# Twenty load widths instead of eleven in a masked softmax

## The chip, the cores and the metric

The kernel runs on one core of one Trainium2 chip. The metric is the device time of one execution in microseconds (us).

## The reference

```python
batch, heads, seq_q, seq_k = 16, 8, 256, 256
x       = randn(batch, heads, seq_q, seq_k)             # float32
lengths = randint(seq_k // 2, seq_k, size=batch)        # 128 to 255

for b in range(batch):
    masked = x[b, :, :, :lengths[b]]
    masked = masked - max(masked, axis=-1)
    e = exp(masked)
    result[b, :, :, :lengths[b]] = e / sum(e, axis=-1)  # the other columns are 0
```

Each batch has 2048 rows of 256 columns, 2 MB. Only the first `lengths[b]` columns of a row count, so the rest need not be read. The draw is fixed: the lengths of batches 0 to 15 are 188, 233, 229, 243, 195, 252, 165, 210, 222, 180, 209, 157, 159, 199, 214 and 248.

## The kernel before

**Tiling.** A batch is one tile of 128 partitions with 16 rows of 256 columns each. `xt` holds eight such tiles (slots). The work goes through 16 positions; `batch_of` says which batch stands at a position: batches 1, 2, 3 and 15 at positions 0 to 3, batches 4 to 14 at positions 4 to 14, and batch 0 at position 15.

**Loads.** SyncE loads position 0 in two halves. GpSimd loads positions 1 to 3 as whole rows (line 196). Positions 4 to 15 are the narrow loads: a loop of six turns (line 205), each with an even and an odd position (`par`). For each, GpSimd waits until the slot's old contents are stored (`s_st[par]`, line 209), reads the batch's length into a register (line 210), and calls `pick` (line 163). `pick` is a binary tree over the list `widths` with the full 256 columns at its end. Each inner node compares the length with a width (line 173); each leaf waits for the landing of the load before last (`s_sw[par]`, line 167) and then issues a DMA of the first w columns of every row (line 168). So the choice is made ahead of the wait for the landing, and behind the wait for the slot. The tree is written out twice in the loop, once for each parity.

**What is not loaded.** Columns from `low` (160) on are filled with zeros once, in slots 4 to 7 (`fill`, line 190); the others hold older numbers. The mask makes a very negative number of all columns behind the length, so that what stands there doesn't matter.

**Compute.** VectorE masks columns 128 to 255 of a tile (`mask`, `clip`, line 248), ScalarE takes the exponential, in part with row sums (lines 374 and 377), VectorE sums the other rows (`total`, line 269), takes reciprocals (line 279) and multiplies a half tile at a time (line 282). The order on VectorE is written out by hand (lines 289 to 304).

**Stores.** SyncE stores each half tile or quarter when VectorE has multiplied it (lines 146 to 156), always whole rows of 256 columns, so their bytes don't depend on the lengths. The last position's stores count on `s_last`, and SyncE's wait for it (line 407; the profile shows it under line 433) is the last of the program.

**After the loop.** A few small instructions check that all sums were in range (lines 310 to 328); with this draw the second, exact pass behind them is not run.

Of the kernel before, what the change touches and what calls it, by code (L numbers as in the profile page):

```python
# [21 lines left out]
def kernel(  # L22
# [28 lines left out]
        return pos + 1 if pos < ahead - 1 else {ahead - 1: 15, 15: 0}.get(pos, pos)  # L51


    widths = list(range(160, 248, 8))
    low = widths[0]
    mid = seq_k // 2
    big = 1.0e30
# [380 lines left out]
```

## Time and profile before

| | before |
|---|---|
| median of 3 runs | 154.69 us (154.58 to 154.7) |
| profiled execution: span, first to last instruction | 152.8 us |
| the profiled execution's own time beside the span | not on the page |
| VectorE (DVE) busy | 134.6 us, 88% |
| ScalarE (ACT) busy | 95.1 us, 62% |
| GpSimd (POOL) busy | 21.3 us, 14% |
| moved by DMA | 61.57 MB, 403 GB/s over the span |
| read from and written to HBM | 27.98 MB, 33.55 MB |

Engine names in the profile: DVE is VectorE, ACT ScalarE, POOL GpSimd, SPq the queue of SyncE and POOLq that of GpSimd. A row of a group gives line, engine, operation, the tiles, the count and the durations. A row of a wait gives the waiting engine and line, what it waited for, the total in us, the count and the longest. A row of a stage gives the stretch, then the busy time of each engine with the count of instructions, the granted TensorE clock, the busy share of the 16 DMA engines and the GB/s they moved. A row of the timeline gives start and duration in us; in brackets is the idle time ahead of it and what ended it. A row of a DMA queue gives packets, MB and the share of the 16 engines' time. A row of DMA issues gives the count, KB each and the us from issue to landing.

### The profile page before, as it was taken

What the parts mean: (1) busy time and instruction counts of PE and PEld (TensorE: products, weight loads), DVE (VectorE), ACT (ScalarE), POOL (GpSimd) and SP (SyncE); (2) the same over time, 40 slices, a digit from 0 to 9 for tenths busy, and PEclk for the clock granted to TensorE, in tenths of its full rate; (3) what the DMA queues carried; (4) which work ended last, traced back from release to release, by engine and by line L of the source; (5) the groups of instructions that cost most, each with busy time, mean ns of one, the idle gap of its engine ahead of it and who ended that gap; (6) DMA issues with size and microseconds to landing.
All of it is one profiled execution on the core that took longest, in us unless ns stands there. A gap on an engine that the chain in (4) does not pass through costs nothing.

```text
span 152.8 us, 818 instructions
## 1 busy us (share of the span) xinstructions
PE 0.3 (0%) x2; PEld 0.2 (0%) x2; DVE 134.6 (88%) x107; ACT 95.1 (62%) x402; POOL 21.3 (14%) x29
## 2 busy tenths in 40 slices
PE   0000000000000000000000000000000000000000
PEld 0000000000000000000000000000000000000000
DVE  1369999999999999999999999999999999999500
ACT  3096699339394967859393939577593939395000
POOL 4962110030303020030300220302000000000000
DMA  4999999999999999999999999999999999999994
GB/s 107 420 446 433 401 435 347 421 445 420 394 397 422 405 421 411 411 409 405 419 411 418 408 399 419 408 410 423 417 421 419 413 420 422 435 435 442 429 410 187
DMA packets 10646, 61.57 MB, mean 403 GB/s; under 512 B 898, under 2 KB 1010, under 8 KB 7058
## 3 DMA queue, kind: packets, MB, share of 16 engines
q1 hardware_dynamic: 5904, 35.65, 56.7%
q0 software_dynamic: 4736, 25.89, 41.9%
q14 instruction: 4, 0.03, 0.1%
q10 hardware_dynamic: 2, 0.00, 0.0%
HBM read 27.98 MB, written 33.55 MB: 403 GB/s over the span
## 4 chain that ended last, share of the span: by engine, by line
DVE 87%; DMA 5%; issue 1%; SPq 0%; PE 0%
DVE xt L282 48%; DVE xt L248 23%; DVE row_sum L269 12%; DMA xt<-in_x_dram 5%; DVE inv_sum L279 3%; DVE ends L317 0%; SPq L145 0%; DVE bad L320 0%; PE count L218 0%; DVE redo L328 0%; SPq L433 0%; SPq L106 0%
## 5 line engine op out<-in xcount | busy, mean ns | idle before, releaser
L377 ACT ACTIVATE xt<-xt 128x256 f32<-128x256 f32 x192 | 76.6, 400 | 0.2 <-DVE xt L248 0.2
L282 DVE TENSOR_TENSOR xt<-xt,inv_sum 128x2048 f32<-128x2048 f32 x32 | 73.3, 2292 | 1.1
L374 ACT ACTIVATE xt<-xt 128x1024 f32<-128x1024 f32 x16 | 16.9, 1056 | 42.8 <-DVE xt L248 42.8
L248 DVE SCALAR_TENSOR_TENSOR xt<-down,len_s,xt 128x2048 f32<-128x2048 f32 (+1 forms) x17 | 37.7, 2219 | 5.0 <-DMA xt<-in_x_dram 5.0
L377 ACT ACTIVATION_READ_ACCUMULATOR xt<-xt 128x1 f32 x192 | 35.9, 187 | 0.0
L168 POOL DMA_DIRECT2D xt<-in_x_dram x12 | 13.2, 1104 | 84.0 <-DMA xt<-in_x_dram 62.3
L269 DVE TENSOR_REDUCE row_sum<-xt 128x4 f32<-128x1024 f32 x16 | 19.4, 1210 | 0.0
L279 DVE RECIPROCAL inv_sum<-row_sum 128x8 f32<-128x8 f32 x32 | 6.3, 198 | 0.5
L191 POOL MEMSET xt<- 128x1536 f32 x4 | 5.4, 1398 | 1.1 <-DVE len_s L239 1.1
L361 ACT ACT_TABLE_LOAD x1 | 1.3, 1283 | 1.6 <-SPq L106 1.6
L196 POOL DMA_DIRECT2D xt<-in_x_dram x3 | 1.8, 590 | 0.0
L231 DVE TENSOR_SCALAR down<-iota_i 128x256 f32<-128x256 int32 x1 | 0.3, 300 | 1.6 <-POOL iota_i L181 1.6
L317 DVE TENSOR_REDUCE ends<-inv_sum 128x1 f32<-128x256 f32 x2 | 0.7, 408 | 0.0
L236 DVE CAST len_b<-word 1x16 bf16<-1x16 int32 x1 | 0.2, 164 | 0.4 <-DMA word<-in_lengths_dram 0.4
L239 DVE TENSOR_SCALAR len_s<-len_f 128x16 f32<-128x16 f32 x1 | 0.2, 176 | 0.3 <-PE len_f L216 0.3
L218 PE MATMUL count<-bad,ones_c 128*1 128x3 bf16 x1 | 0.2, 165 | 140.8 <-DVE bad L320 140.8
L181 POOL IOTA iota_i<- 128x256 int32 x1 | 0.3, 331 | 0.6 <-SPq L106 0.6
L328 DVE TENSOR_REDUCE redo<-count 1x1 f32<-1x3 f32 x1 | 0.1, 150 | 0.3 <-PE count L218 0.3
L320 DVE TENSOR_SCALAR bad<-ends 128x1 bf16<-128x1 f32 x3 | 0.3, 150 | 0.0
L187 POOL MEMSET seed<- 1x1 f32 x2 | 0.2, 225 | 0.0
L218 PEld LDWEIGHTS count<-bad,ones_c 128*1 128x1 bf16 x1 | 0.1, 79 | 140.8 <-DVE bad L320 140.8
L361 ACT ACTIVATE warm<-const-float32-0.0 128x1 f32<-128x1 f32 x1 | 0.2, 204 | 0.0
(10 smaller groups left out, 1.1 us busy)
## 6 DMA issues: line engine op xcount, KB each, us to landing
out_dram<-xt SPq DMA_DIRECT2D x20, 1024.0 KB
xt<-in_x_dram POOLq DMA_DIRECT2D x4, 2048.0 KB, 16.3
out_dram<-xt SPq DMA_DIRECT2D x15, 512.0 KB
xt<-in_x_dram POOLq DMA_DIRECT2D x3, 1728.0 KB, 16.7
out_dram<-xt SPq DMA_DIRECT2D x2, 2048.0 KB
xt<-in_x_dram POOLq DMA_DIRECT2D x2, 1600.0 KB, 16.0
xt<-in_x_dram POOLq DMA_DIRECT2D x2, 1280.0 KB, 14.7
xt<-in_x_dram SPq DMA_DIRECT2D x2, 1024.0 KB, 6.4
```

Of the source, the lines that this page charges most:

```text
L168: nc.gpsimd.dma_start(out=xt[:, slot, :, :w], in_=x_n[:, b, :, :w]).then_inc(s_sw[par], 16)
L191: nc.gpsimd.memset(xt[:, b, :, low:], 0.0).then_inc(s_fill, 1)
L196: nc.gpsimd.dma_start(out=xt[:, b], in_=x_f[batch_of(b)]).then_inc(s_sw[b - 1] if b < 3 else s_ld[2], 16)
L218: nc.tensor.matmul(count, lhsT=ones_c, rhs=bad, start=True, stop=True).then_inc(s_count, 1)
L248: return nc.vector.scalar_tensor_tensor(out=t, in0=down[:, None, lo:hi].to_broadcast([P, s.stop - s.start, hi - lo]), scalar=len_s[:, batc ...
L269: nc.vector.tensor_reduce(out=row_sum[:, b % slots, :lump], in_=xt[:, b % slots, :lump, :], op=ALU.add, axis=AX,).then_inc(s_exp[0], 1)
L279: step(nc.vector.reciprocal(out=inv_sum[:, b, s], in_=row_sum[:, b % slots, s]))
L282: nc.vector.tensor_tensor(out=t, in0=t, in1=inv_sum[:, b, s, None].to_broadcast([P, half, seq_k]), op=ALU.mult,).then_inc(s_out, 1)
L317: step(nc.vector.tensor_reduce(out=ends[:, k : k + 1], in_=values, op=op, axis=AX))
L361: nc.scalar.activation(out=warm, in_=nc.const_aps.tensor(0.0, (P, 1), F32), func=EXP)
L374: nc.scalar.activation(out=e, in_=e, func=EXP).then_inc(s_lump, 1)
L377: ins = nc.scalar.activation(out=e, in_=e, func=EXP, accum_out=row_sum[:, slot, j : j + 1])
```

## The change

The list of widths is 160, 164, ... 236 (20 entries) instead of 160, 168, ... 240 (11 entries). The full row of 256 columns stays as the last leaf, so the tree has 21 leaves instead of 12, and lengths of 237 to 240 are now loaded as full rows. `pick` itself is not changed; `low` stays 160.

```diff
-    widths = list(range(160, 248, 8))
+    widths = list(range(160, 240, 4))
     low = widths[0]
```

| position | 4 | 5 | 6 | 7 | 8 | 9 | 10 | 11 | 12 | 13 | 14 | 15 |
|---|---|---|---|---|---|---|---|---|---|---|---|---|
| length | 195 | 252 | 165 | 210 | 222 | 180 | 209 | 157 | 159 | 199 | 214 | 188 |
| columns before | 200 | 256 | 168 | 216 | 224 | 184 | 216 | 160 | 160 | 200 | 216 | 192 |
| columns after | 196 | 256 | 168 | 212 | 224 | 180 | 212 | 160 | 160 | 200 | 216 | 188 |
| comparisons before | 3 | 3 | 4 | 4 | 3 | 4 | 4 | 4 | 4 | 3 | 4 | 4 |
| comparisons after | 4 | 3 | 4 | 4 | 5 | 4 | 4 | 5 | 5 | 4 | 4 | 5 |

## The prediction

> **What bounds the kernel now.** I read the page's header, its DMA line and queue table first, then the waits, then VectorE's timeline and the table by stage.
>
> ```profile
> span 152.8 us, 818 instructions
> DMA  4999999999999999999999999999999999999994
> q1 hardware_dynamic: 5904, 35.65, 56.7%
> q0 software_dynamic: 4736, 25.89, 41.9%
> q14 instruction: 4, 0.03, 0.1%
> ```
>
> The two data queues took 56.7% + 41.9% = 98.6% of all sixteen DMA engines' time over the whole span: q1 is SyncE's stores and the first load, q0 is GpSimd's loads. From the second slice to the last but one no slice falls below nine tenths. This is a kernel whose transfer engines have nearly no free time. VectorE looks just as full:
>
> ```profile
> DVE xt L248 <- DMA xt<-in_x_dram: 5.0, 2, 3.5
> 9.26 1.29 DVE L248 SCALAR_TENSOR_TENSOR xt<-down,len_s,xt 128x1024 f32<-128x1024 f32 x1 [1.52 <-DMA xt<-in_x_dram]
> 131.53 2.34 DVE L248 SCALAR_TENSOR_TENSOR xt<-down,len_s,xt 128x2048 f32<-128x2048 f32 x1
> 140.15 2.29 DVE L282 TENSOR_TENSOR xt<-xt,inv_sum 128x2048 f32<-128x2048 f32 x1
> ```
>
> Only two waits of VectorE for a load are there, 5.0 us in sum, and the second ends at 9.26 us, which is the mask of the second half of position 0. All later masks found their data landed. The last multiplication ends at 140.15 + 2.29 = 142.44 us. What follows decides which of the two full resources sets the end:
>
> ```profile
> SPq L433 <- DMA out_dram<-xt: 4.2, 1, 4.2
> 46.00:116.00 70.00, 0.00 (x0) 0.00 (x0) 69.17 (x50) 48.19 (x208) 9.20 (x8) 1.00 1.02 413
> 128.00:150.00 22.00, 0.17 (x1) 0.08 (x1) 15.39 (x18) 9.21 (x43) 0.00 (x0) 1.00 1.01 429
> 146.00:150.00 4.00, 0.00 (x0) 0.00 (x0) 0.00 (x0) 0.00 (x0) 0.00 (x0) 1.00 1.00 422
> 150.00:152.80 2.80, 0.00 (x0) 0.00 (x0) 0.00 (x0) 0.00 (x0) 0.00 (x0) 1.00 0.26 108
> ```
>
> In the stage rows the last two numbers are the DMA share and GB/s. From 146 to 150 us all compute engines are idle and the DMA share is still 1.00; the engines empty in the last row (0.26 of 2.80 us is 0.7 us, so about at 150.7 us on average), and SyncE's last wait, 4.2 us long, is for a store. At 142.44 us only the last half batch, 1 MB, becomes ready, which at 422 GB/s is 2.5 us; the engines worked 8.3 us more. So a backlog of stores stood in the queue, VectorE is not what ends the run, and the end is when the DMA engines have done all their work. With a share of 1.00 to 1.02 in every stage, engine time taken off anywhere comes off the end at full value, and engine time added comes on in full.
>
> **What the change does to the data.** A load of w columns moves 128 partitions x 16 rows x 4 bytes x w, that is 8 KB for each column. With the drawn lengths, positions 4 to 15 load 200, 256, 168, 216, 224, 184, 216, 160, 160, 200, 216 and 192 columns; the issue rows show those sizes:
>
> ```profile
> xt<-in_x_dram POOLq DMA_DIRECT2D x3, 1728.0 KB, 16.7
> xt<-in_x_dram POOLq DMA_DIRECT2D x2, 1600.0 KB, 16.0
> xt<-in_x_dram POOLq DMA_DIRECT2D x2, 1280.0 KB, 14.7
> xt<-in_x_dram POOLq DMA_DIRECT2D x1, 1536.0 KB, 21.0
> xt<-in_x_dram POOLq DMA_DIRECT2D x1, 1472.0 KB, 17.0
> xt<-in_x_dram POOLq DMA_DIRECT2D x1, 1344.0 KB, 13.4
> ```
>
> With steps of 4, position 4 (length 195) loads 196 instead of 200, positions 7 and 10 (210, 209) load 212 instead of 216, position 9 (180) loads 180 instead of 184 and position 15 (188) loads 188 instead of 192. The other seven keep their width; no drawn length is in 237 to 240, where the new list would load a full row. Five loads lose 4 columns, 32 KB each: 163,840 bytes of 61.57 MB, and every row that is shortened ends 16 bytes earlier.
>
> **The price of those bytes.** q0 moved 25.89 MB in 0.419 x 152.8 = 64.0 us of all engines, 404 GB/s. At that price the saving is 163,840 / 404,000 = 0.41 us; at the 429 GB/s of the stage that has only stores it is 0.38 us. That is the lower end: -0.41 us. It needs a row of 784 bytes to be cheaper than one of 800 in proportion to its bytes. All rows of this trace are whole multiples of 32 bytes (8 columns), so none shows whether a piece of 16 bytes is cheaper, free or dearer.
>
> The upper end comes from what being cut into rows costs at all. Stage 46 to 116 holds the narrow loads, stage 128 to 150 stores alone. Per engine time they move 413/1.02 = 405 and 429/1.01 = 425 GB/s. The 28.9 MB of the first stage would have taken 68.0 us of engine time at 425 instead of 71.4: 3.4 us for about seven narrow loads that land there (positions 8 to 14), 0.48 us a load, an estimate that puts all of it on the rows. If an odd end costs a row as much again, the five loads add 5 x 0.48 = +2.4 us. Between -0.41 and +2.4 the nearest row is that of the loads' time to landing: 1600 KB took 16.0 us, 1472 KB 17.0 and 1536 KB 21.0, so a difference of 2% in size is not what these rows react to. I take 0 for the price: neither a gain nor a loss.
>
> [...]
>
> **The price of the choice.** The tree goes from 12 to 21 leaves. With the drawn lengths the paths of the twelve loads hold 44 comparisons before and 51 after.
>
> ```profile
> L173 POOLq COMPARE_BRANCH  x47: 34/40/55, 11.1 to 105.3; - x47
> POOL xt L168 <- DMA xt<-in_x_dram: 62.3, 9, 12.9
> POOL xt L168 <- issue: 15.5, 2, 8.5
> 106.21 1.15 POOL L168 DMA_DIRECT2D xt<-in_x_dram  x1 [6.97 <-issue]
> DMA to landing us min/median/max: 13.4/16.8/21.0
> ```
>
> Seven more at 55 ns are 0.4 us over the run, 0.8 us if a taken branch costs as much again. They stand ahead of the wait in the leaf, where GpSimd waited 62.3 us for earlier loads in nine of the cases. In the two cases put down to "issue" the choice may not be covered; the last load (106.21 us) is one, and its path grows by one comparison. It lands by 106.21 + 21.0 = 127.2 us at the latest and its mask starts at 131.53, so 4.3 us of slack cover a tenth of a microsecond. If that cover were gone, VectorE would wait that tenth, still under the 8.3 us by which the engines outlast it. Nothing else is queued on GpSimd behind the choice but the next choice. Cost on the path: 0.
>
> **The price of the code.** 18 more leaves and 18 more comparisons make GpSimd's program longer. q14 fetched 4 packets of 8 KB in the span; at q1's 35.65 MB / (0.567 x 152.8 us x 16) = 25.7 bytes per ns one holds one engine 0.32 us. One more packet on an engine that finishes last would add 0.32 us; on another engine nothing. I take 0, with +0.32 as the upper bound.
>
> Sum: 152.8 + 0 + 0 + 0 = 152.8 us of span. The page gives no time beside its span; the median of the three runs is 154.69, 1.89 us more, which lies outside the span and is left as it is: 154.69 us.
>
> **The rivals.**
>
> Bytes count. If the engines are paid by the byte, 0.38 to 0.41 us come off an end that the DMA engines set: 154.3 us. For it speak the share of 1.00 and the backlog; against it, only that no row has a 16-byte rest. This is just over the 0.2% (0.31 us) that a measurement of this kernel can tell from no change. Chance 0.26.
>
> Odd ends cost. The engine or the memory treats a half-filled last piece as something extra, once a row, 2048 rows a load, in five loads. Its price is between 0 and +2.4 us; the middle is +1.2, 155.9 us. It decides from 0.31 us, that is from 0.06 us a load or an eighth of what being cut into rows costs now. For it speaks that rows already cost 5% of rate against whole partitions; against it, that row lengths of 21, 23, 25 and 27 times 32 bytes land no later than those of even ones. Chance 0.27.
>
> Code is fetched more often. [...] A fetch more once costs 0.32 us at most (155.0). Chance of over 0.31 us by either, 0.08.
>
> [...] That is the forecast, 0.39.
>
> **How the numbers follow.** Forecast 154.69 us with 0.39, within 0.2%. Faster by over 0.2%: 0.26 (bytes). Slower: 0.27 + 0.08 = 0.35. The forecast's own range is 154.4 to 155.0. The range for 8 in 10 takes in the byte price, 154.69 - 0.41 and a little spread, 154.2, and reaches up through the middle of the odd-end case to 156.2, leaving out the upper third of it and the worst of the fetches, some 0.15 together.
>
> **What would show it.** In the profile after: q0 should show 25.73 MB and five issue rows of 1696 (twice), 1568, 1504 and 1440 KB. If the forecast holds, q0's share stays at 41.9% within a tenth while its bytes fall by 0.6%, and VectorE still has no wait after 9.3 us. If bytes count, q0's share falls to 41.6%. If odd ends cost, q0's share rises (by 0.8 points for +1.2 us) and GB/s in stage 46 to 116 falls below 413. If code costs, q14 has more than 4 packets. A wait of VectorE for a load after 9.3 us would show the slack argument wrong.

## The result, and the profile after

The changed kernel takes 155.11 us (median of 22 runs) against 154.60 us before (22 runs): ratio 1.003, 95% interval 1.0017 to 1.0042. It is slower by 0.3%, about 0.46 us (0.51 by the medians). Against "no change within 0.2%" the forecast was wrong, though the time lies in the range. The same kernel was run once more beside other experiments, with 1.002 to 1.004 expected: the medians were 155.00 against 154.56 us, but the ratio came out as 1.0013 (0.9993 to 1.0032), an interval that takes in no change; 4 of the 23 runs of the kernel before took 155.2 to 155.6 us there. The profiled executions of the changed kernel agree with each other: spans of 153.3 and 153.4 us against 152.8 us.

The page of the changed kernel, the lines that answer to those of before (queue rows: packets, MB, share of 16 engines' time):

```profile
span 153.3 us, 827 instructions
DMA  4999999999999999999999999999999999999993
q1 hardware_dynamic: 5904, 35.65, 56.8%
q0 software_dynamic: 4736, 25.72, 41.7%
q14 instruction: 5, 0.04, 0.1%
```

From its waits, DMA issues and the table by stage (the last two numbers are DMA share and GB/s):

```profile
DVE xt L248 <- DMA xt<-in_x_dram: 5.0, 2, 3.3
```

```profile
xt<-in_x_dram POOLq DMA_DIRECT2D x2, 1696.0 KB, 16.1
xt<-in_x_dram POOLq DMA_DIRECT2D x1, 1504.0 KB, 21.1
```

```profile
46.00:116.00 70.00, 0.00 (x0) 0.00 (x0) 69.17 (x50) 48.27 (x208) 9.22 (x8) 1.00 1.02 411
128.00:150.00 22.00, 0.17 (x1) 0.08 (x1) 15.48 (x19) 9.29 (x43) 0.00 (x0) 1.00 1.01 429
150.00:153.30 3.30, 0.00 (x0) 0.00 (x0) 0.00 (x0) 0.00 (x0) 0.00 (x0) 1.00 0.23 94
```

The change does what it says: 0.16 MB less on q0, the new sizes in the issue rows. VectorE still waits for loads only twice, 5.0 us in sum, so the end is set by the DMA engines as before. Share times span gives the engines' time of each queue. Its step is 0.1% of the span, 0.15 us. For the loads (q0) it was 64.0 us (0.419 x 152.8) and is 63.9; for the stores (q1), whose bytes are the same, it was 86.6 us and is 87.1 (64.1 and 87.0 us in the second profile). Summed over the records of the single packets, the loads went from 64.05 to 63.89 us, 0.17 less, and the stores from 86.73 to 87.03, 0.31 more. So the loads gained next to nothing from their lost bytes, and the stores became dearer.

The last stage row shows a second thing. Share times length is how long the average engine still worked after 150 us: 0.73 us before (0.26 x 2.80), 0.76 us after (0.23 x 3.30). The average engine finished at the same time, while the span grew by 0.5 us: the slowest engine, which the last store waits for, fell further behind the others. The stretch from 151.3 us shows it, first before, then after:

```profile
151.30:152.00 0.70, 0.00 (x0) 0.00 (x0) 0.00 (x0) 0.00 (x0) 0.00 (x0) 1.00 0.00 0
151.30:152.00 0.70, 0.00 (x0) 0.00 (x0) 0.00 (x0) 0.00 (x0) 0.00 (x0) 1.00 0.03 12
```

12 GB/s for 0.70 us are 8 KB: one packet, on one engine, where before none was started any more. And q14 has 5 packets, not 4.

Of the signs that the prediction listed, the fifth instruction packet and the lower rate in 46 to 116 us came. The sign in q0's share misled: it fell to 41.7%, near the 41.6% that was to mean that bytes count, in part because the span is longer; the loads' time fell by 0.17 us and not by 0.4.

Two theories were tested: the odd row ends cost (the data), or GpSimd's longer program costs (the code). They can be parted, since the width of a leaf's transfer need not be the width with which the length is compared.

### The profile page after: what moved, and what is told of

The parts are those of the page before. It is cut to its first block, busy times and chain, and to the rows that moved or that the text cites. A ratio compares the mean times of both kernels' runs of the same rounds, so it can differ in the third digit from the quotient of the medians.

```text
span 153.3 us, 827 instructions
## 1 busy us (share of the span) xinstructions
PE 0.3 (0%) x2; PEld 0.2 (0%) x2; DVE 134.7 (88%) x107; ACT 95.1 (62%) x402; POOL 21.3 (14%) x29
## 3 DMA queue, kind: packets, MB, share of 16 engines
q1 hardware_dynamic: 5904, 35.65, 56.8%
q0 software_dynamic: 4736, 25.72, 41.7%
## 4 chain that ended last, share of the span: by engine, by line
DVE 87%; DMA 5%; issue 1%; SPq 0%; PE 0%
DVE xt L282 48%; DVE xt L248 23%; DVE row_sum L269 12%; DMA xt<-in_x_dram 5%; DVE inv_sum L279 3%; DVE ends L317 0%; SPq L145 0%; DVE bad L320 0%; PE count L218 0%; DVE redo L328 0%; SPq L433 0%; SPq L106 0%
```

## The experiments

### The changed rows with the old size of program, twice

```diff
-    widths = list(range(160, 248, 8))
+    widths = [160, 168, 180, 188, 196, 200, 212, 216, 224, 232, 240]
```

> The changed kernel's rows with the old size of program: 11 widths picked so that all drawn lengths load the columns of the changed kernel (196, 212, 180, 212, 188 where it changed), 12 leaves. If the odd row ends cost the 0.3% (0.46 us), this is slower by as much, about 155.1 against 154.6 us, with 4 instruction packets. If the longer program costs it, this is 154.2 to 154.6 us, ratio 1.000 or below, down to 0.9975 if the bytes are paid.

> The changed rows with 12 leaves once more, for a narrower number: with 5 odd loads where 11 cost 0.36%, in proportion 1.0016; by the first run 1.0004 to 1.001.

Measured: ratio 1.0004 (0.9992 to 1.0016), then 1.0011 (1.0002 to 1.002), 154.69 against 154.56 us. Page and last stage of the second run:

```profile
span 153.0 us, 818 instructions
q1 hardware_dynamic: 5904, 35.65, 56.9%
q0 software_dynamic: 4736, 25.72, 41.7%
q14 instruction: 4, 0.03, 0.1%
```

```profile
150.00:153.00 3.00, 0.00 (x0) 0.00 (x0) 0.00 (x0) 0.00 (x0) 0.00 (x0) 1.00 0.27 112
```

Loads 63.8 us, stores 87.1 us: 0.2 less and 0.4 more than before, close to the changed kernel. The average engine works 0.81 us after 150, against 0.73. The data is at most a part of the 0.3% (the first interval takes in no change, the second only just does not), and it shows as slightly more work.

### The changed tree with the rows of before, twice

```diff
-    widths = list(range(160, 248, 8))
+    widths = list(range(160, 240, 4))
...
                 w = ws[0]
+                w8 = -(-w // 8) * 8
...
-                    out=xt[:, slot, :, :w], in_=x_n[:, b, :, :w]
+                    out=xt[:, slot, :, :w8], in_=x_n[:, b, :, :w8]
```

> The changed kernel's tree of 21 leaves, but each leaf's DMA rounds its width up to a multiple of 8 columns, so the transfers are those of the kernel before. If the longer program costs the 0.46 us, this is about 155.1 us, ratio 1.003, with 5 or more instruction packets. If the odd ends cost it, the ratio is 1.000.

> The changed tree with the rows of before once more: if it makes up what the odd ends leave of the change's 0.3%, 1.0012 to 1.002; if the program's length costs nothing below the edge, 1.000.

Measured: ratio 1.0012 (0.999 to 1.0034), then 1.0014 (1.0005 to 1.0023), 154.78 against 154.56 us. Page and last stage of the second run:

```profile
span 153.1 us, 827 instructions
q1 hardware_dynamic: 5904, 35.65, 56.5%
q0 software_dynamic: 4736, 25.89, 41.8%
q14 instruction: 5, 0.04, 0.1%
```

```profile
150.00:153.10 3.10, 0.00 (x0) 0.00 (x0) 0.00 (x0) 0.00 (x0) 0.00 (x0) 1.00 0.18 77
```

Here the two queues took no more than before (64.0 and 86.5 us), and the average engine worked only 0.56 us after 150, less than the 0.73 of before. Yet the run is longer. The time is not in the engines' work but in its spread: one engine is late. The fifth instruction packet is there. The instruction packets of 8 KB take 0.31 us in the spans before and after the change (309 to 312 ns). By the records of the single data packets, the last engine ends at least 0.27 us behind the next one in all seven profiles with a fifth instruction packet of 8 KB and at most 27 leaves (the changed kernel, with 0.44 us, this one, and those with a longer program below), and 0.01 to 0.15 us behind it in the eight without.

The two halves in their second runs, +0.11% and +0.14%, make +0.25%, which agrees with the 0.3% of both, and with the 0.13% of its repeat within the intervals. The spans add up as well: 152.8 us before, 153.0 with the data alone, 153.0 and 153.1 with the code alone, 153.3 and 153.4 with both.

### More odd ends, and whole pieces, without the longer program

```diff
                 w = ws[0]
+                wt = w - 4 if w < seq_k else w      # and w - 8, w - 1
...
-                    out=xt[:, slot, :, :w], in_=x_n[:, b, :, :w]
+                    out=xt[:, slot, :, :wt], in_=x_n[:, b, :, :wt]
```

> The 12 leaves of before, but each of the 11 narrow loads leaves off the last 4 columns of its width, needed or not: 11 odd row ends of 16 bytes instead of the change's 5, 360 KB less. If bytes are paid, 0.84 us faster, ratio 0.9945. If whole pieces of 32 bytes are paid, 1.000. If an odd end costs something of its own, the small excess of the data-only run (0.04%) doubles to about 1.001, and packets of the stores beside these loads are longer than in the kernel before.

> The 12 leaves of before, but each of the 11 narrow loads leaves off the last 8 columns, needed or not: rows 32 bytes shorter and still whole multiples of 32, 721 KB less. If the DMA engines set the end and a whole piece is paid, 721 KB at 429 GB/s are 1.68 us off: 152.9 us, ratio 0.989. If a load's price were not the engines' time, 1.000.

> The 12 leaves of before; each of the 11 narrow loads leaves off its last column, needed or not: row ends of 28 bytes in a last piece of 32, 90 KB less. Leaving off 4 columns cost 0.36%. If any row that is not a multiple of 32 bytes pays, this is slower by about as much, 1.002 to 1.005. If only a half piece pays, or if the 0.36% came from elsewhere, 1.000.

The runs with 4 and 8 columns less leave out columns that some batches need; they serve for the time alone. Measured: 4 columns less, ratio 1.0036 (1.0014 to 1.0059), 155.09 us, well over the 1.001 expected for a cost of odd ends. 8 columns less, 0.9882 (0.9854 to 0.991), 153.0 us. 1 column less, 1.0065 (1.0052 to 1.0078), 155.53 us. The pages, in that order:

```profile
span 153.4 us, 818 instructions
q1 hardware_dynamic: 5904, 35.65, 57.0%
q0 software_dynamic: 4736, 25.53, 41.7%
```

```profile
span 151.3 us, 818 instructions
q1 hardware_dynamic: 5904, 35.65, 57.3%
q0 software_dynamic: 4736, 25.17, 41.4%
```

```profile
span 153.9 us, 818 instructions
q1 hardware_dynamic: 5904, 35.65, 56.7%
q0 software_dynamic: 4736, 25.80, 41.9%
```

With 4 columns less the loads take 64.0 us for 25.53 MB, what they took for 25.89 MB: 16 bytes off a row are not paid back at all. With 8 columns less they take 62.6 us, 1.4 us less, and the run is 1.6 us shorter by the medians, where 721 KB at 429 GB/s are 1.68 us: 32 bytes off a row are paid, and the DMA engines do set the end. Nor are 4 bytes paid back: with 1 column less, rows that end in a rest of 28 bytes, the loads take 64.5 us, more than with the column.

A second cost is in q1. The stores, unchanged, take 87.4 us beside 16-byte ends and 87.3 us beside 28-byte ends, against 86.6 us before and 86.7 us beside whole pieces. Here the stores beside loads with odd row ends are slower by 0.6 to 0.8 us of engine time. The records of the single packets say the same: in 46 to 116 us a store packet of 4 KB took 162.9 ns on average before and 163.5 beside whole pieces, 164.1 and 164.4 beside five odd loads (data alone, changed kernel), 166.0 and 165.6 beside eleven (16 and 28 bytes). The stage 46 to 116 of the three, in the same order, and the last stage of the first and the third:

```profile
46.00:116.00 70.00, 0.00 (x0) 0.00 (x0) 69.17 (x50) 48.15 (x208) 9.20 (x8) 1.00 1.02 408
150.00:153.40 3.40, 0.00 (x0) 0.00 (x0) 0.00 (x0) 0.00 (x0) 0.00 (x0) 1.00 0.31 130
```

```profile
46.00:116.00 70.00, 0.00 (x0) 0.00 (x0) 69.17 (x50) 48.19 (x208) 9.20 (x8) 1.00 1.02 412
```

```profile
46.00:116.00 70.00, 0.00 (x0) 0.00 (x0) 69.17 (x50) 47.55 (x205) 9.20 (x8) 1.00 1.02 407
150.00:153.90 3.90, 0.00 (x0) 0.00 (x0) 0.00 (x0) 0.00 (x0) 0.00 (x0) 1.00 0.41 174
```

At the same share of 1.02 the rate falls from 412 GB/s beside whole pieces to 408 and 407; of the first, about 3 GB/s against the 413 of before are bytes no longer moved, an estimate from seven loads of 32 KB less in 70 us. The average engine works 1.05 and 1.60 us after 150, against 0.73 before, that is 0.3 and 0.9 us more where the span grew by 0.6 and 1.1: half or more of this cost is work of all engines, unlike that of the code.

### The choice itself

```diff
+                with ExitStack() as deep:
+                    for k in range(4):
+                        deep.enter_context(nc.gpsimd.If(v_len <= 1000 + k))
                     pick(v_len, ...)
```

> The kernel before with four more comparisons, always true, ahead of each choice: 48 more comparisons are run (the change adds 7) with 8 more instructions in the program (the change adds 90). If the time goes with the comparisons run, up to 1.003; if with the length of the program or not at all, 1.000.

Measured: ratio 0.9999 (0.9991 to 1.0008), 154.55 us. 48 comparisons more cost nothing; those that the change adds don't either. They are eight, not seven: the table ahead of the prediction has 3 for position 5 after the change, but by `pick` a length of 252 now takes 4. The page of this run counts 5 instruction packets, but 0.03 MB as before: the fifth has 32 bytes.

### A longer program ahead of the loop

```diff
+        never = length(POOL, word[0:1, 0:1])
+        with nc.gpsimd.If(never <= 0):
+            for _ in range(86):
+                nc.gpsimd.memset(spare, 0.0)
         with nc.Fori(16, 16 * (batch // 2 - 1), 16, engines=[POOL]) as landed:
```

> The kernel before with 86 instructions in a branch that is never taken, ahead of the loop: GpSimd's program is as long as that of the change, but the loop with its 12 leaves keeps its size. If the whole program's length costs the 0.14% (one more instruction packet on a DMA engine), 1.001 to 1.002 with 5 packets; if it is the loop's own size, 1.000 with 4.

Measured: ratio 1.0027 (1.0015 to 1.0038), 155.10 us, somewhat over the 1.001 to 1.002 expected for the whole program's length. Page and last stage:

```profile
span 153.4 us, 820 instructions
q1 hardware_dynamic: 5904, 35.65, 56.6%
q0 software_dynamic: 4736, 25.89, 41.7%
q14 instruction: 5, 0.04, 0.1%
```

```profile
150.00:153.40 3.40, 0.00 (x0) 0.00 (x0) 0.00 (x0) 0.00 (x0) 0.00 (x0) 1.00 0.18 77
```

The loop, its 12 leaves and the rows are those of before; the 86 instructions never run, only the test ahead of them does. The fifth instruction packet comes, the average engine works 0.61 us after 150 and the span grows by 0.6 us. So the small price of the code needs no larger loop and no more leaves; a longer program is enough.

### Fewer and more leaves

All five have the rows of before; the trees of 24 to 40 leaves round each transfer up as above.

```diff
+    widths = [160, 168, 184, 192, 200, 216, 224]                                # 8 leaves
+    widths = sorted([*range(160, 240, 4), 162, 186, 210])                       # 24
+    widths = sorted([*range(160, 240, 4), *range(162, 210, 8)])                 # 27
+    widths = sorted([*range(160, 240, 4), *range(162, 234, 8)])                 # 30
+    widths = list(range(160, 238, 2))                                           # 40
```

> Only the 8 leaves that the drawn lengths use, with the transfers of the kernel before: a shorter program. If the program's length costs step by step, this is faster than before, ratio 0.998 to 1.000, with 4 or fewer instruction packets. If the odd ends cost it, 1.000.

> 24 leaves with the rows of before. The edge between 21 leaves (154.8 us, 5 packets) and 30 (172.9 us, 31 packets) is a step in the loop's size, so this is either about 154.8 or about 172; if the price grew evenly from 21 on, about 160.

> 27 leaves with the rows of before, to place the edge: about 154.8 us with 5 packets, or about 172 us with some 30; 165 to 167 if the price grew evenly.

> 30 leaves with the transfers of the kernel before. The run with 40 leaves took 172.1 us, that with 21 about 154.7. If the price of the program's length grows evenly, some 163 us; if there is an edge where the loop no longer fits what is held, either about 155 us with 5 or 6 instruction packets, or about 172 with some 30.

> A tree of 40 leaves in steps of 2 columns, each DMA rounded up to a multiple of 8 columns: the transfers of the kernel before, and twice the added program. If the program's length costs, the time rises with it: 1.006 or more (155.5 us), with more instruction packets than the 5 of the changed kernel, and more still if the loop no longer fits what is held. If the odd ends cost it, 1.000.

| leaves | median us | ratio to before | instruction packets in the span |
|---|---|---|---|
| 8 | 154.59 | 1.0 (0.9983 to 1.0017) | 4 |
| 12 (before) | 154.56 to 154.60 | 1 | 4 |
| 21 | 154.78 | 1.0014 (1.0005 to 1.0023) | 5 |
| 24 | 155.04 | 1.0019 (0.9998 to 1.0041) | 5 |
| 27 | 154.97 | 1.0021 (1.0004 to 1.0038) | 6 (0.04 MB: five, and one of 32 bytes) |
| 30 | 172.94 | 1.1167 (1.1127 to 1.1208) | 31 |
| 40 | 172.08 | 1.1127 (1.1099 to 1.1155) | 31 |

From 21 to 27 leaves the price stays within the intervals, with five full packets each time. Then there is a step, between 27 and 30 leaves. Page, waits and one stage with 30 leaves (the line numbers are one higher):

```profile
span 171.0 us, 832 instructions
DMA  4999999999999969999799999999489999992795
q14 instruction: 31, 0.25, 0.4%
```

```profile
DVE xt L249 <- DMA xt<-in_x_dram: 26.6, 8, 8.3
```

```profile
60.00:80.00 20.00, 0.00 (x0) 0.00 (x0) 15.85 (x13) 10.87 (x48) 2.27 (x2) 1.00 0.94 350
```

31 packets are 27 more than before, between four and five for each of the six turns; the author reads this count as a loop that is fetched again every turn. GpSimd then issues its loads late (the last at 129.7 us, before at 106.2), VectorE waits for loads eight times (26.6 us), and for the first time the DMA engines have gaps (0.94). This is the third rival of the prediction, code fetched more often. It costs some 18 us, and the engines' time for the packets is not what costs: q14's 0.4% of 171.0 us is 0.7 us. The time goes with the late loads. The change with its 21 leaves and 5 packets stays short of it; why the step lies where it does was not shown.

## Why the prediction was wrong

**What bounds the kernel: right.** The DMA engines set the end. Taking 721 KB in whole pieces off the loads made the run shorter by 1.6 us by the medians (1.8 by the ratio), where 721 KB at 429 GB/s are 1.68 us.

**The bytes: half right.** The loads' own price for 16 bytes off a row was taken as 0, and it is: 64.0 us of engine time with and without, over 11 loads. The step that failed is that this was the whole price. The second rival named the odd end as a cost of its own, but looked for it in the rows of the loads (a rise of q0's share). It lies in the stores beside them, 0.3 to 0.4 us of engine time for five loads, partly made up by 0.2 us on the loads; in time +0.11%, 0.17 us (0.04% in the first of the two runs). The rival was bounded at 2.4 us and put at 1.2 in the middle, seven times too much. The argument against it, that lengths of 21, 23, 25 and 27 pieces land no later than even ones, spoke of whole pieces only.

**The choice: right.** The additional comparisons (eight, where the prediction counted seven) cost nothing, and neither do 48.

**The code: mis-sized.** Its price was taken as 0 with +0.32 us as the upper bound, for one packet on an engine that finishes last. It measured +0.14% (0.05 to 0.23%), 0.22 us: one more packet, and the slowest engine later while the average one is not. The mechanism was named and the bound held for the middle value; the value taken was the wrong end of it. In the changed kernel the last engine ends 0.44 us behind the next (151.81 against 151.37 us), more than the 0.31 us of one instruction packet, where before it was 0.04 (151.27 against 151.23): the delay of one engine was not averaged away.

**The sum.** Two terms put at 0 were 0.17 and 0.22 us, each inside the 0.2% (0.31 us) that was called no change, and both of one sign. Together they are 0.25%, and 0.3% was measured (0.13% in the repeat). The rivals were each weighed alone, none as a sum of two small costs. "The worst of the fetches", which the range leaves out, has no price that a run shows; what the runs showed is 4 packets at 12 leaves, 5 of 8 KB at 21 to 27, and 31 packets and some 18 us at 30.

**Left open.** Why odd ends make neighbouring stores slower, and why 28-byte ends cost more than 16-byte ends, no run here tells. Nor was it shown on which engine the fifth instruction packet fell. In the profiles with that packet GpSimd also issues its narrow loads 0.7 to 1.1 us later from the third one on (the third at 34.1 us in the code-only run and 33.9 in the changed kernel, against 33.0), and no run parts this from the packet's own time; beside the 28-byte ends the loads were issued up to 1.0 us later too, without a fifth packet, and the last engine ended only 0.01 us behind the next. A store packet of 8 KB takes 0.31 us as well, so the gap at the end alone does not tell which kind of packet held up the late engine; that it comes with the fifth instruction packet in all seven profiles points to that one. The run with the longer program ahead of the loop lost 0.27%, 0.42 us by the middle value; its interval (0.23 to 0.59 us) takes in both the 0.22 us of the longer tree and the 0.32 us of one packet, so whether it costs more than one packet is open.

## What to carry to other kernels

Where the DMA engines set the end, as here, trim transfers by steps that are paid back: 32 bytes off each row of eleven loads took 1.6 us off the run, 4 columns (16 bytes) added 0.5 us instead, and beside such odd ends another queue's transfers were slower (87.4 us of engine time for 86.6). Code that is unrolled into a loop for a fine choice had a price too: 0.1 to 0.3% here with one more 8 KB instruction packet, and 11% of the time with 31 instruction packets in place of 4, so look at the instruction queue's packets and bytes before adding leaves. When several costs are each too small to measure, add them up before calling the change neutral.

## What the runs showed of the hardware

The row ends of the loads changed the price of another queue's transfers: 86.6 us of engine time for the same 35.65 MB of stores became 87.1 us beside five odd loads and 87.4 us beside eleven. Rows ending 4 bytes short of a whole 32 bytes cost more than rows ending 16 bytes short (0.65% against 0.36%; the intervals overlap slightly, but the loads' engine time, 64.5 against 64.0 us, points the same way). One more 8 KB instruction packet (0.31 us) came with a last engine at least 0.27 us behind the next at the end, 0.44 us in the changed kernel, against 0.01 to 0.15 us without it. The kernel ran with 5 instruction packets of 8 KB in the span at 21 to 27 leaves, and with 31 at 30 and 40 leaves, at 11% more time.
